# One GpSimd power for the roots of keys and queries, and output weights whose loads are written ahead of their splits

## The chip, the cores and the metric

The kernel runs on one core of one Trainium2 chip. The metric is device time in microseconds; lower is better. In the profile the engines are PE (TensorE, matrix products), PEld (its weight loads), DVE (VectorE), ACT (ScalarE), POOL (GpSimd) and SP (SyncE, which issues most DMAs).

## The reference

One decoder layer is computed for a prompt group (512 tokens behind 16 meta tokens) and a sample group (8 sequences of 8 tokens with 2048 cached positions each). Differential attention and a gated delta rule read the same projection of the normalised input; their outputs are projected, gated, merged and sent through one output projection; a gated feed-forward part follows. All is float32. What the change touches, cut to its core:

```
def l2norm(x):
    return x * rsqrt(sum(x * x, axis=-1) + 1e-6)

gq = l2norm(gq) * GDN_DK ** -0.5          # queries of the delta rule, 4 heads of 128
gk = l2norm(gk)                           # keys
...
mix = sigmoid(gate_a) * (o_a @ w_branch_a) + sigmoid(gate_b) * (o_b @ w_branch_b)
x = x + rmsnorm(mix @ w_out, ln_mix_post)
```

## The kernel before, in words

Every product in float32 is built from three rounded ones: a weight tile is loaded raw, ScalarE casts it to its high part, DVE subtracts that for the low part (`split`, lines 314 to 316), and PE multiplies high by high, high by low and low by high (line 273 records all of them). Raw tiles (`wraw`, 128x512) come through SP's queue into three buffers in rotation (`load_w`, lines 308 to 312).

The work is written as two streams of generators that a planner merges by the PE work that each has used: `main` makes the prompt attention and then the delta rule head by head (`gdn`), `rest` makes the sample attention over the cached pages, the sixteen gates and one branch projection (`branch_a`). What the streams emit is then ordered once more for every engine, by when its operands are expected. So the order in which the program is written and the order in which an engine finds its instructions are two things. Each engine works off its own order strictly.

The delta rule of a head (`gdn_chain`, heads counted 0 to 3) starts at the scaling of keys and queries. The keys are transposed to rows (`kn`) and ScalarE sums the squares of keys and queries into `gss`, ten columns: five for the keys, five for the queries, of which columns 0 to 3 are the four chunks of the prompt and column 4 is the tail of 80 rows (samples and meta tokens). `rsqrt` (lines 382 to 385) is a scaling on DVE and a power of -0.5 on GpSimd; it was called once for the keys and once for the queries, into the halves of `grr`. From the keys' half DVE makes `kc` (line 811) and scales `kn` with it (line 814 for the tail, 815 for the chunks); from the queries' half it makes `cq` (line 813). PE then transposes `kn` back (line 421), the Gram products follow, DVE solves the blocks of sixteen (`gdn_base`, lines 953 to 1009, whose results are `xyt` for the tail and `xy` for the chunks), and PE goes on from those. At the same time the next head's projection is convolved on DVE (`cy`, lines 670 to 672, ended by a tanh on ScalarE). `er` (line 833) is the queries times their decays, `vn` (lines 801 and 806) the scaled values, `zk` and `grhs` small copies for later.

The output weights: `branch_a` and `mix` call `wout_ahead` (lines 1560 to 1563) behind each of their steps. It loads a quarter of the first half of `w_out` as two raw tiles and splits them at once into `owhi` and `owlo`. Each step of `branch_a` and `mix` also takes one raw tile for its own branch weights. `out_proj` loads the second half in the same manner.

Of the kernel before, what the change touches and what calls it, by code (L numbers as in the profile page):

```python
# [29 lines left out]
EPS = 1e-6  # L30
# [121 lines left out]
class Body:  # L152
# [39 lines left out]
    def run(self):  # L192
# [13 lines left out]
        with ExitStack() as sm:  # L206
            with ExitStack() as s1:
# [3 lines left out]
                with ExitStack() as s2:  # L211
# [12 lines left out]
                        self.gdn_consts(tmp)  # L224
                    self.news = self.chain = self.spare = False

                    swo, self.wo0, self.wo_next = ExitStack(), [], 0

                    def main():
                        head = {}  # L230
# [503 lines left out]
    def gdn_chain(self, h, st):  # L734
        nc, pool, a, o = self.nc, self.gpool, self.a, self.o
        q, kt, vt = st["q"], st["kt"], st["vt"]
# [43 lines left out]
        ss = self.t(pool, [128, 2, 5], "gss")  # L780
# [24 lines left out]
            self.transpose(pv[:, i], vt[:, 128 * i : 128 * i + 128])  # L805
        nc.vector.tensor_tensor(out=vn[:, 0:4], in0=pv, in1=cols(self.hsb), op=ALU.mult)
        rr = self.t(pool, [128, 2, 5], "grr")
        for e in range(2):
            self.rsqrt(rr[:, e], ss[:, e], 0.25, EPS, 128, 5)
        kc = self.t(pool, [128, 5], "kc")  # L810
        nc.vector.tensor_tensor(out=kc, in0=rr[:, 0], in1=self.hsb[:, :, h], op=ALU.mult)
        cq = self.t(pool, [128, 5], "cq")
# [6 lines left out]
        p = self.ps("t")  # L819
# [3 lines left out]
        p = self.ps4("t")  # L823
# [25 lines left out]
        p = self.ps("g")  # L849
# [13 lines left out]
        p = self.ps("g")  # L863
# [4 lines left out]
        p = self.ps("g")  # L868
# [3 lines left out]
        p = self.ps("g")  # L872
# [26 lines left out]
        for i in range(4):  # L899
            sl = slice(128 * i, 128 * i + 128)  # L900
            p = self.ps("g")
# [9 lines left out]
            p = self.ps("g")  # L911
# [4 lines left out]
            p = self.ps("g")  # L916
# [5 lines left out]
            p = self.ps("g")  # L922
# [18 lines left out]
        p = self.ps4("t")  # L941
# [4 lines left out]
        for dst, src in (((0, SEQ), p.rearrange("p c t -> p (c t)")), ((CS, CM), pt[:, 0:NS]), ((CM, NQ), pt[:, 78:80])):  # L946
            sl = slice(*dst)
# [610 lines left out]
        yield 2.0  # L1558

    def wout_ahead(self):  # L1560
        if self.wo0 and self.wo_next < 4:
            self.load_wout(self.wo0, 0, self.wo_next)
            self.wo_next += 1

    def mix(self):
# [15 lines left out]
    def wout_tiles(self, pool, half):  # L1581
        return tuple(self.t(pool, [128, 8, 512], f"ow{part}{half}", F32R) for part in ("hi", "lo"))

    def load_wout(self, wo, half, q):
        hi, lo = wo
        sl = slice(128 * q, 128 * q + 128)
        for k in (0, 4):
            raw = self.load_w(self.a["w_out"][0][128 * k : 128 * k + 512, 512 * half + 128 * q : 512 * half + 128 * q + 128])
            self.split(hi[:, k : k + 4, sl], lo[:, k : k + 4, sl], raw)

    def out_proj(self, pool, wo0, swo, sm):
        nc, a, f = self.nc, self.a, self.f
# [691 lines left out]
```

## Time and profile before

| | us |
|---|---|
| median of 3 runs | 1135.75 |
| lowest and highest | 1135.46, 1139.98 |
| the profiled execution | 1136.37 |
| its span, first to last instruction | 1134.6 |
| busy: PE, DVE, ACT, POOL | 1112.5, 729.3, 524.7, 225.8 |

The profiled execution took 1.8 us more than its span, which lies around the instructions, and 0.6 us more than the median. A row of a view of instructions has the start in us from the span's start, the duration in us, engine, line, operation, output and inputs, shapes, how many of a kind were merged, and in brackets how long the engine had stood idle before it and what ended that. Rows with three numbers in ns give the shortest, middle and longest duration of a group. Since PE is busy nearly throughout, what is looked for is the rest: the places where it waits.

### The profile page before, as it was taken

Reading aid. Unit: us, or ns where it says so; the run is one execution under the profiler, and the core shown is the slowest. Engines: PE = TensorE matmul, PEld = TensorE weight load, DVE = VectorE, ACT = ScalarE, POOL = GpSimd, SP = SyncE. Lnnn points to the kernel's source line nnn. Section 1 sums busy time; section 2 is a strip of 40 time slices with the busy share of each in tenths; the row PEclk is TensorE's granted clock in tenths of the full one; section 3 lists DMA queues with packets and bytes.
Section 4 is the critical chain, followed back from the end, with each engine's and each line's share of the span. In section 5 each row is a group of like instructions: output and inputs, shape, how many; then the busy total and the mean of one; then the engine's idle time right before and its main releaser. Section 6 shows DMA issues by size and latency. Waiting matters only on the chain.

```text
span 1134.6 us, 22730 instructions
## 1 busy us (share of the span) xinstructions
PE 1112.5 (98%) x8263; PEld 976.8 (86%) x8263; DVE 729.3 (64%) x1891; ACT 524.7 (46%) x1264; POOL 225.8 (20%) x344
## 2 busy tenths in 40 slices
PE   8999999999999999999999999999999999999997
PEld 6987887787787787689999987899999999988886
DVE  5456666696486377375335575599999999752315
ACT  5244544464365365352324244464555555842311
POOL 3122221020120020010000003344444454300000
PEclk9999999999999999999999999999999999999999
DMA  6376336837846866733234344333333332333213
GB/s 193 83 235 199 102 92 200 261 103 251 246 147 224 283 178 223 251 87 87 50 90 118 105 146 135 102 102 95 94 95 95 95 100 84 116 108 108 84 48 120
DMA packets 167610, 156.97 MB, mean 138 GB/s; under 512 B 12540, under 2 KB 123715, under 8 KB 167498
## 3 DMA queue, kind: packets, MB, share of 16 engines
q1 hardware_dynamic: 162833, 147.14, 42.5%
q0 software_dynamic: 3264, 5.16, 1.5%
q10 hardware_dynamic: 1400, 3.22, 0.9%
q8 instruction: 65, 1.06, 0.4%
q14 instruction: 48, 0.39, 0.1%
HBM read 145.60 MB, written 9.88 MB: 137 GB/s over the span
## 4 chain that ended last, share of the span: by engine, by line
PE 82%; DVE 7%; issue 3%; ACT 3%; POOL 3%; DMA 2%; SPq 0%; DVEq 0%; POOLq 0%; ACTq 0%
PE ps_d L273 32%; PE ps_t L273 20%; PE ps_g L273 16%; PE ps_s L273 7%; PE ps_t L421 6%; ACT KT L1421 1%; PE ps_m L273 1%; DVE wlo L316 1%; DVE cy L672 1%; POOL grr L385 1%; DMA wraw<-in_w_ffn_in 1%; DMA page<-in_cache_v 0%; DVE gf L1745 0%; DVE fy L1926 0%; DVE row L992 0%
## 5 line engine op out<-in xcount | busy, mean ns | idle before, releaser
L273 PE MATMUL ps_d<-xhi,whi 128*128 128x256 f32 (+2 forms) x704 | 217.3, 309 | 0.6 <-ACT xhi L315 0.5
L273 PE MATMUL ps_d<-xhi,wlo 128*128 128x256 f32 (+2 forms) x704 | 213.0, 303 | 0.5 <-POOL wlo L316 0.5
L273 PE MATMUL ps_d<-xlo,whi 128*128 128x256 f32 (+2 forms) x704 | 212.4, 302 | 0.3 <-DVE xlo L316 0.3
L316 DVE TENSOR_TENSOR wlo<-wraw,whi 128x512 fp32r<-128x512 f32 x190 | 143.5, 772 | 107.2 <-ACT whi L315 106.3
L315 ACT CAST whi<-wraw 128x512 fp32r<-128x512 f32 x194 | 116.5, 621 | 163.7 <-PE ps_d L273 69.4
L273 PEld LDWEIGHTS ps_d<-xhi,whi 128*128 128x128 f32 x704 | 133.1, 189 | 6.2 <-issue 3.8
L273 PEld LDWEIGHTS ps_d<-xlo,whi 128*128 128x128 f32 x704 | 133.4, 190 | 3.2 <-issue 2.4
L273 PEld LDWEIGHTS ps_d<-xhi,wlo 128*128 128x128 f32 x704 | 133.2, 189 | 2.4 <-issue 1.0
L316 DVE TENSOR_TENSOR lw<-sw,hw 128x512 fp32r<-128x512 f32 x76 | 69.8, 918 | 5.2 <-ACT hw L315 5.2
L1421 ACT COPY KT<-ps_t 128x512 f32<-128x512 f32 x106 | 57.2, 603 | 31.6 <-PE ps_t L421 31.1
L421 PE MATMUL ps_t<-consts,page 128*128 128x128 f32 x512 | 67.8, 279 | 0.5
L273 PE MATMUL ps_t<-fhit,hw 128*128 128x290 f32 x228 | 68.1, 299 | 0.1
L273 PE MATMUL ps_t<-flot,hw 128*128 128x290 f32 x228 | 67.7, 297 | 0.0
L273 PE MATMUL ps_t<-fhit,lw 128*128 128x290 f32 x228 | 67.7, 297 | 0.0
L421 PEld LDWEIGHTS ps_t<-consts,page 128*128 128x128 f32 x512 | 55.5, 140 | 14.1 <-issue 7.0
L315 ACT CAST hw<-sw 128x512 fp32r<-128x512 f32 x76 | 46.7, 617 | 18.5 <-PE ps_g L273 12.2
L273 PEld LDWEIGHTS ps_t<-fhit,hw 128*128 128x128 f32 x228 | 43.0, 189 | 0.4 <-DVE p L1949 0.4
L273 PEld LDWEIGHTS ps_t<-flot,hw 128*128 128x128 f32 x228 | 43.3, 190 | 0.0
L273 PEld LDWEIGHTS ps_t<-fhit,lw 128*128 128x128 f32 x228 | 43.1, 189 | 0.0
L1924 ACT ACTIVATE fy<-fpre,fw 128x592 f32<-128x592 f32 x22 | 19.5, 884 | 46.3 <-DVE fpre L1884 46.3
L1926 DVE SCALAR_TENSOR_TENSOR fy<-fpre,fw,fy 128x592 f32<-128x592 f32 x44 | 36.5, 829 | 1.0 <-ACT fy L1924 0.3
L273 PE MATMUL ps_s<-page,pT 128*32 128x256 f32 x512 | 35.1, 385 | 2.0 <-DMA page<-in_cache_v 1.8
(691 smaller groups left out, 2870.0 us busy)
## 6 DMA issues: line engine op xcount, KB each, us to landing
page<-in_cache_k SPq DMA_DIRECT2D x128, 256.0 KB, 4.4
page<-in_cache_v SPq DMA_DIRECT2D x128, 256.0 KB, 4.2
wraw<-in_w_in SPq DMA_DIRECT2D x88, 256.0 KB, 3.1
wraw<-in_w_ffn_in SPq DMA_DIRECT2D x50, 256.0 KB, 3.0
wraw<-in_w_down SPq DMA_DIRECT2D x44, 256.0 KB, 2.8
raw<-in_w_ffn_in SPq DMA_DIRECT2D x38, 256.0 KB, 2.9
wraw<-in_w_out SPq DMA_DIRECT2D x16, 256.0 KB, 3.2
x<-in_x_prompt SPq DMA_DIRECT2D x4, 512.0 KB, 6.8
```

Of the source, the lines that this page charges most:

```text
L273: return self.nc.tensor.matmul(out, lhsT, rhs, **kw).ins
L315: self.nc.scalar.copy(hi, raw)
L316: (eng or self.nc.vector).tensor_tensor(out=lo, in0=raw, in1=hi.bitcast(F32), op=ALU.subtract)
L385: nc.gpsimd.tensor_tensor(out=dst, in0=dst, in1=self.mhalf[:rows, :n], op=ALU.pow)
L421: self.nc.tensor.transpose(out, in_, self.ident[:k, :k])
L672: nc.vector.scalar_tensor_tensor(out=y, in0=pre[:, j : j + n], scalar=self.cw[:, ch, 24 + j : 25 + j], in1=y, op0=ALU.mult, op1=ALU.add)
L1421: copy(kt[:, :, 128 * j : 128 * j + 128], tp)
L1924: nc.scalar.activation(y, pre[:, 0:592], AF.Identity, bias=fw[:, m, 19:20], scale=fw[:, m, 16:17])
L1926: nc.vector.scalar_tensor_tensor(out=y, in0=pre[:, j : j + 592], scalar=fw[:, m, 16 + j : 17 + j], in1=y, op0=ALU.mult, op1=ALU.add)
```

## The change

Two edits. The first calls `rsqrt` once on all ten columns instead of twice on five. The second separates the loads of the output weights from their splits: a step now splits the two raw tiles that the step before had asked for, and then asks for the next two; one step more is needed in all, so the count goes to five. `out_proj` keeps load and split together.

```
-        for e in range(2):
-            self.rsqrt(rr[:, e], ss[:, e], 0.25, EPS, 128, 5)
+        self.rsqrt(rr.rearrange("p e c -> p (e c)"), ss.rearrange("p e c -> p (e c)"), 0.25, EPS, 128, 10)
...
     def wout_ahead(self):
-        if self.wo0 and self.wo_next < 4:
-            self.load_wout(self.wo0, 0, self.wo_next)
+        if self.wo0 and self.wo_next < 5:
+            self.split_wout(self.wo0, self.wo_raws)
+            self.wo_raws = self.load_wout(0, self.wo_next) if self.wo_next < 4 else []
             self.wo_next += 1
...
-    def load_wout(self, wo, half, q):
-        hi, lo = wo
-        sl = slice(128 * q, 128 * q + 128)
-        for k in (0, 4):
-            raw = self.load_w(self.a["w_out"][0][128 * k : 128 * k + 512, 512 * half + 128 * q : 512 * half + 128 * q + 128])
-            self.split(hi[:, k : k + 4, sl], lo[:, k : k + 4, sl], raw)
+    def load_wout(self, half, q):
+        c0 = 512 * half + 128 * q
+        return [(q, k, self.load_w(self.a["w_out"][0][128 * k : 128 * k + 512, c0 : c0 + 128])) for k in (0, 4)]
+
+    def split_wout(self, wo, raws):
+        for q, k, raw in raws:
+            self.split(*(e[:, k : k + 4, 128 * q : 128 * q + 128] for e in wo), raw)
...
-            self.load_wout(wo[1], 1, q)
+            self.split_wout(wo[1], self.load_wout(1, q))
```

What the engines get of it: the second edit changes no row of any engine's order, neither the loads on SP nor the casts on ScalarE nor the subtractions on DVE, and no row waits for another engine or queue than before. The first edit moves rows at the four heads. On DVE at head 0, from the first conv operation of the next tile to the scaled keys, before:

```order
L670 TENSOR_SCALAR cy_3445<-pre_3434,cw_666 128x616
L384 TENSOR_SCALAR grr_3460<-gss_3335 128x5
L811 TENSOR_TENSOR kc_3465<-grr_3460,hsb_635 128x5
L672 SCALAR_TENSOR_TENSOR cy_3445<-pre_3434,cw_666,cy_3445 128x616
L813 TENSOR_SCALAR cq_3467<-grr_3460 128x5
L814 TENSOR_SCALAR kn_3337<-kn_3337,kc_3465 80x128
L672 SCALAR_TENSOR_TENSOR cy_3445<-pre_3434,cw_666,cy_3445 128x616
L815 TENSOR_TENSOR kn_3337<-kn_3337,kc_3465 128x512
```

and with the change:

```order
L384 TENSOR_SCALAR grr_3460<-gss_3335 128x10
L832 TENSOR_TENSOR er_3311<-q_2267,er_3311 128x576
L672 SCALAR_TENSOR_TENSOR cy_3445<-pre_3434,cw_666,cy_3445 128x616
L810 TENSOR_TENSOR kc_3463<-grr_3460,hsb_635 128x5
L812 TENSOR_SCALAR cq_3465<-grr_3460 128x5
L672 SCALAR_TENSOR_TENSOR cy_3445<-pre_3434,cw_666,cy_3445 128x616
L813 TENSOR_SCALAR kn_3337<-kn_3337,kc_3463 80x128
L672 SCALAR_TENSOR_TENSOR cy_3445<-pre_3434,cw_666,cy_3445 128x616
L814 TENSOR_TENSOR kn_3337<-kn_3337,kc_3463 128x512
```

The product er, which stood behind the scaled keys, now stands right behind the scaling, and one cy more stands ahead of the keys; the scaling of the keys' five columns, six rows ahead of the first row shown before, is gone. At head 1 the copy tailT moves from between cq and kn to just behind the scaling, and a small copy (zk) stands between cq and kn instead. At head 2 the keys' scaling stood ahead of er and the queries' one three rows later, behind vn (line 801) and a cy; the one now stands behind er, vn and that cy, and tailT follows it. On DVE at head 3, from the values to the scaled keys, before:

```order
L384 TENSOR_SCALAR grr_7284<-gss_7208 128x5
L811 TENSOR_TENSOR kc_7289<-grr_7284,hsb_635 128x5
L801 TENSOR_SCALAR vn_7211<-ps_t_7245,hsb_635 80x128
L384 TENSOR_SCALAR grr_7284<-gss_7208 128x5
L814 TENSOR_SCALAR kn_7210<-kn_7210,kc_7289 80x128
L815 TENSOR_TENSOR kn_7210<-kn_7210,kc_7289 128x512
L813 TENSOR_SCALAR cq_7291<-grr_7284 128x5
L316 TENSOR_TENSOR wlo_7495<-wraw_7490,whi_7494 128x512
```

and with the change:

```order
L801 TENSOR_SCALAR vn_7205<-ps_t_7239,hsb_635 80x128
L384 TENSOR_SCALAR grr_7278<-gss_7202 128x10
L858 COPY grhs_7941<-vn_7205 16x128
L316 TENSOR_TENSOR wlo_7487<-wraw_7482,whi_7486 128x512
L810 TENSOR_TENSOR kc_7281<-grr_7278,hsb_635 128x5
L812 TENSOR_SCALAR cq_7283<-grr_7278 128x5
L813 TENSOR_SCALAR kn_7204<-kn_7204,kc_7281 80x128
L814 TENSOR_TENSOR kn_7204<-kn_7204,kc_7281 128x512
```

vn, a small copy and one subtraction of weights have moved ahead of kc. On PE the one move of more than two products is behind the blocks of head 1, where ps_s is a score of the sample attention and ps_d the projection for the next head. Before:

```order
L273 MATMUL ps_d_5802<-xhi_6_84,wlo_5796 128x256
L273 MATMUL ps_d_5802<-xhi_6_84,whi_5795 128x256
L273 MATMUL ps_s_5155<-KT_5233,qb_315 32x256 x4
L273 MATMUL ps_s_5155<-KT_5217,qb_315 32x256 x4
L421 MATMUL ps_t_5274<-consts_66,xyt_4936 80x80
L273 MATMUL ps_t_5279<-consts_66,xy_4938 128x32 x4
```

and with the change:

```order
L273 MATMUL ps_d_5798<-xhi_6_84,wlo_5792 128x256
L421 MATMUL ps_t_5270<-consts_66,xyt_4932 80x80
L273 MATMUL ps_d_5798<-xhi_6_84,whi_5791 128x256
L273 MATMUL ps_s_5151<-KT_5229,qb_315 32x256 x4
L273 MATMUL ps_s_5151<-KT_5213,qb_315 32x256 x4
L273 MATMUL ps_t_5275<-consts_66,xy_4934 128x32 x4
```

The transposition of xyt has moved ahead of one projection product and eight scores; xy has stayed behind them. On GpSimd the two powers of a head are one row at the same place.

More of the change, by code (lines that the diff above doesn't have):

```diff
@@ L225, in run @@
                     self.news = self.chain = self.spare = False
-                    swo, self.wo0, self.wo_next = ExitStack(), [], 0
+                    swo, self.wo0, self.wo_next, self.wo_raws = ExitStack(), [], 0, []
                     def main():
```

## The prediction

> **What bounds the kernel now.** First the page's busy times and its chain of waits:
>
> ```profile
> PE 1112.5 (98%) x8263; PEld 976.8 (86%) x8263; DVE 729.3 (64%) x1891; ACT 524.7 (46%) x1264; POOL 225.8 (20%) x344
> PE 82%; DVE 7%; issue 3%; ACT 3%; POOL 3%; DMA 2%; SPq 0%; DVEq 0%; POOLq 0%; ACTq 0%
> ```
>
> TensorE (PE) is busy for 1112.5 of 1134.6 us, so everything that can ever be saved without removing products is its idle time, about 22 us. An edit counts only by the idle time of PE that it adds or takes away. Where that may be I read from the busy times by stage (the columns are PE, weight loads, VectorE (DVE), ScalarE, GpSimd (POOL)):
>
> ```profile
> 230.00:260.00 30.00, 29.85 (x258) 25.57 (x260) 28.81 (x86) 19.82 (x61) 6.26 (x13) 1.00 0.38 123
> 510.00:595.00 85.00, 85.00 (x648) 82.69 (x647) 36.62 (x115) 27.83 (x74) 2.70 (x3) 1.00 0.30 76
> 595.00:680.00 85.00, 84.39 (x593) 80.63 (x592) 51.31 (x90) 33.06 (x61) 0.00 (x0) 1.00 0.42 122
> ```
>
> Where the first head's roots are taken (230 to 260 us) DVE is nearly as full as PE, 28.81 of 30. After the last head's roots PE has no idle time at all (85.00 of 85), so what PE loses or wins before 510 us arrives at the end undiminished. The granted clock is 1.00 in all three.
>
> **The output weights: nothing.** Their stage is 595 to 690 us. ScalarE does wait for these loads, but PE does not:
>
> ```profile
>   DMA wraw<-in_w_out: 10.8, 11
> PE ps_d L273 <- DVE gt L1534: 0.6, 1, 0.6
> ```
>
> The first row is ScalarE's idle time before its casts of w_out, 10.8 us in 11 waits; the second is the only wait of PE between 590 and 690 us. So a perfect early load would be worth at most 0.6 us. And the edit does not even do that: the rows of every engine in this stage are the same in both kernels, one by one (tile numbers apart): the order in which the program is written is not the order in which the engines get it. The 16 loads on SP's queue, the 16 casts on ScalarE and the 16 subtractions on DVE stand at the same places, between the same branch weights, waiting for the same engines. With three raw buffers in rotation, a load cannot start before its buffer is free, wherever the program writes it. Cost: 0, both ways.
>
> **The roots: the price of one power of ten columns.** The trace has no power of ten columns. It has these:
>
> ```profile
> L385 POOL TENSOR_TENSOR r<-r,mhalf x10: 546/554/927, 5.5 to 738.1; 128x1 f32<-128x1 f32 x8, 80x1 f32<-80x1 f32 x1, 66x1 f32<-66x1 f32 x1
> L385 POOL TENSOR_TENSOR grr<-grr,mhalf x8: 1162/1203/1797, 239.4 to 501.7; 128x5 f32<-128x5 f32 x8
> L554 POOL TENSOR_TENSOR sqb<-beta,half x1: 3543/3543/3543, 52.3 to 52.3; 128x20 f32<-128x20 f32 x1
> ```
>
> One column takes 0.55 us, five 1.16 at the least, twenty 3.54. The bounds for ten are therefore 1.16 and 3.54. From one to five a column costs (1.16 - 0.55)/4 = 0.15, from five to twenty (3.54 - 1.16)/15 = 0.16. I take 1.16 + 5 x 0.16 = 1.97 us. The Trainium skill (GPSIMD Engine Reference, section 3.1) gives about 2.6 cycles an element at 1.2 GHz for two-input elementwise work. Estimated from that page, five more columns would cost 11 ns and a power of ten still 1.2 us; the 0.15 us a column of this trace does not bear it out for a power, and it is kept as a rival below.
>
> The longest of the eight is 1.80 us. When it is long shows in the third head:
>
> ```profile
> 417.54 0.75 DVE L833 TENSOR_TENSOR er<-q,er 128x576 f32<-128x576 f32 x1
> 417.71 2.92 POOL L385 TENSOR_TENSOR grr<-grr,mhalf 128x5 f32<-128x5 f32 x2 [2.21 <-DVE grr L384]
> 419.47 1.17 POOL L385 TENSOR_TENSOR grr<-grr,mhalf 128x5 f32<-128x5 f32 x1
> 419.46 0.86 DVE L672 SCALAR_TENSOR_TENSOR cy<-pre,cw,cy 128x616 f32<-128x616 f32 x1
> ```
>
> Of the pair, the second took 1.17 us and so the first 2.92 - 1.17 = 1.75. The first began 0.17 us behind a DVE product with two operands in SBUF and was 0.57 us late; the second began together with one and was not. So I add 0.57 us where DVE already runs such an operation.
>
> Now head by head: when the scaled keys (kn, line 815) are ready before and after, and when PE wants them. Steps between DVE starts come from these rows of the first head: 0.08 for a five-column operation, 0.19 for the small kn, 0.77 for cy, 0.68 to the end of kn.
>
> ```profile
> 240.51 0.18 DVE L384 TENSOR_SCALAR grr<-gss 128x5 f32<-128x5 f32 x1
> 241.97 0.17 DVE L813 TENSOR_SCALAR cq<-grr 128x5 f32<-128x5 f32 x1 [0.33 <-POOL grr L385]
> 242.05 0.27 DVE L814 TENSOR_SCALAR kn<-kn,kc 80x128 f32<-80x128 f32 x1
> 242.24 0.85 DVE L672 SCALAR_TENSOR_TENSOR cy<-pre,cw,cy 128x616 f32<-128x616 f32 x1
> 243.01 0.68 DVE L815 TENSOR_TENSOR kn<-kn,kc 128x512 f32<-128x512 f32 x1
> 245.08 0.67 PE L421 MATMUL ps_t<-consts,kn 80*128 80x80 f32 x5
> ```
>
> *Head 0.* Before, kn is ready at 243.69 and PE takes it at about 245.2: no wait. After, the wide scaling stands at 240.43 (0.08 earlier, a small one ahead of it is gone), the power starts 0.25 later as in the other heads and ends at 242.65; kc, cq, cy, small kn, cy, kn follow in the new order and end at 245.26. PE loses 0.1. But er now stands right behind the scaling, as at 417.54, so I count the 0.57 here: **+0.7**. Queued on DVE behind the waiting kc are the cy of the next conv tile and the tail copy, for which ScalarE's tanh waits; they come some 0.2 later and PE's loss covers them.
>
> ```profile
> 326.00 0.23 DVE L384 TENSOR_SCALAR grr<-gss 128x5 f32<-128x5 f32 x2
> 329.22 0.17 DVE L813 TENSOR_SCALAR cq<-grr 128x5 f32<-128x5 f32 x1 [0.98 <-POOL grr L385]
> 329.54 0.27 DVE L814 TENSOR_SCALAR kn<-kn,kc 80x128 f32<-80x128 f32 x1
> 329.95 0.26 PE L421 MATMUL ps_t<-consts,kn 80*128 80x80 f32 x1 [1.24 <-DVE kn L814]
> ```
>
> *Head 1.* Here PE really waits, 1.24 us, for kn, and DVE's order makes kn wait for the second power as well, since cq stands ahead of it. After: scaling 326.00, power 326.25 to 328.22, kc 328.26, cq, one small copy, kn at 328.52 instead of 329.54: **-1.0**. What is late next is the same transposition, for 0.2 us. But later in this head the order of PE changes too: the transposition of xyt moves ahead of nine products.
>
> ```profile
> 354.20 0.28 PE L273 MATMUL ps_d<-xhi,whi 128*128 128x256 f32 x1
> 354.78 0.24 DVE L998 TENSOR_TENSOR xyt<-xc,consts 80x80 f32<-80x80 f32 x1
> 355.56 0.27 PE L421 MATMUL ps_t<-consts,xyt 80*80 80x80 f32 x1
> 355.77 1.05 PE L273 MATMUL ps_t<-consts,xy 128*128 128x32 f32 x8
> ```
>
> xyt is ready at 355.02, and PE would now want it at 354.20 instead of 355.56. It stands still until 355.06, then does the nine products (ps_d and ps_s, 1.1 us) and comes to xy at about 356.35 instead of 355.77: **+0.6**. DVE and PE are earlier by the same 1.0 here, so that this does not depend on it.
>
> ```profile
> 418.46 0.85 DVE L672 SCALAR_TENSOR_TENSOR cy<-pre,cw,cy 128x616 f32<-128x616 f32 x1
> 421.72 0.68 DVE L815 TENSOR_TENSOR kn<-kn,kc 128x512 f32<-128x512 f32 x1
> 422.29 0.88 PE L421 MATMUL ps_t<-consts,kn 80*128 80x80 f32 x5
> 417.63 0.19 ACT L800 ACTIVATION_READ_ACCUMULATOR gjunk<-ps_t 80x1 f32 x1
> ```
>
> *Head 2.* Before, the keys' root began at 417.45 without the queries' sums. After, vn stands ahead and waits for ScalarE's last sum (417.82), cy follows (418.11), the scaling comes at 418.88, the power runs 419.13 to 421.10, then kc, cq, cy, small kn, and kn ends at 422.94 instead of 422.40. PE wants it at 422.4: **+0.5**.
>
> ```profile
> 499.81 0.19 ACT L800 ACTIVATION_READ_ACCUMULATOR gjunk<-ps_t 80x1 f32 x1
> 501.69 0.68 DVE L815 TENSOR_TENSOR kn<-kn,kc 128x512 f32<-128x512 f32 x1
> 502.52 0.67 PE L421 MATMUL ps_t<-consts,kn 80*128 80x80 f32 x5
> 503.43 0.17 DVE L813 TENSOR_SCALAR cq<-grr 128x5 f32<-128x5 f32 x1 [1.06 <-POOL grr L385]
> ```
>
> *Head 3.* Before, kn came from the first power alone and ended at 502.37, just ahead of PE; the second power (awaited at 503.43) held up only cq and two weight subtractions. After, vn waits for the last sum (500.00), the scaling is at 500.29, the power 500.54 to 502.51, kn ends at 503.58. PE loses **+0.9**. One weight subtraction, with both operands in SBUF, now starts with the power; I count its 0.57 too: **+1.5**.
>
> The four scalings fewer on DVE (4 x 0.08 us) lie beside PE's work and count nothing; if that cover were gone they would be worth 0.3 us. Other swaps on PE move one or two products among independent ones; the only wait of that kind in the trace is 0.2 us (for dtbig_up), and I cost them at 0.
>
> Sum: 0.7 - 1.0 + 0.6 + 0.5 + 1.5 = **+2.3 us** on the profiled execution: 1136.4 becomes 1138.7, and the median of the runs shown, 1135.75, becomes **1138.0**. As a formula: +1.1 on time (0.1 - 1.0 + 0.6 + 0.5 + 0.9), and 4 us for each us by which the power is longer than 1.97.
>
> **The rivals.**
> A. A power of ten costs what five cost (1.18 us). Against it speak the three rows of powers. Heads 0 and 2 then lose nothing, head 1 gains its whole wait of 1.24, xyt costs 0.6, head 3 about 0.1: -0.5, 1135.2 us.
> B. Slower: the power is starved by DVE through a whole row of operations (er and cy back to back, copy and subtraction) and takes as long as twenty columns, 3.5 us. Then 1.1 + 4 x 1.5 = +7.1, 1142.9 us. It decides, beyond 0.5%, from 3.1 us a power on. For it: kn's wait hangs on this one instruction in all heads. Against: the longest delay seen is 0.6 us.
> C. The reverse: a power that began first holds DVE off until it ends. Then in heads 1 and 2 the cy behind the scaling (0.77) comes after the power instead of beside it: +2.3 + 1.5 = 3.8, 1139.6 us. Against it: cy at 419.46 took its usual 0.86 beside a power. The Trainium skill (SBUF — State Buffer, section "Who interferes with whom") says so: the port pair that the two share goes to whichever starts first for its whole instruction, and the other fully blocks. By that rule the longer power would cost DVE more, 3.8 in the sum; the late power at 417.71 agrees with it, the unhindered cy at 419.46 does not.
> D. The losses are absorbed, since PE and the chain wait for each other further on: 0, 1135.8 us. Against it: PE's 85.00 of 85 behind head 3.
> E. The output weights do arrive earlier and take away PE's 0.6: 1137.4 us. The unchanged orders speak against it.
>
> **How the numbers follow.** Forecast 0.62, A 0.08, B 0.07, C 0.10, D 0.08, E 0.05. The range goes from A with the xyt stall missing as well (-1.1, 1134.6) to C with all four powers late (1.1 + 4 x 0.57 + 1.5 = 4.9, 1140.7): 1134.5 to 1141.0, leaving out B. Half a per cent is 5.7 us, about what a measurement of this kernel can tell from no change. Only B reaches it, with a margin for what I do not see: slower 0.08, faster 0.02, same 0.90.
>
> **What would show it.** Right: four powers of 128x10 near 2.0 us, or 2.5 in heads 0 and 3; PE waiting for kn 0.2 us in head 1 and 0.5 to 1.5 in heads 0, 2 and 3; a new wait of PE for xyt near 0.8; ScalarE still idle about 11 us before the casts of w_out. Wrong: powers above 3 us, PE waits for kn in none of the heads, or any difference behind 595 us other than a shift.

## The result, and the profile after

The changed kernel takes **1141.03 us** (median of 8 runs, 1139.82 to 1142.91); the kernel before, run beside it, 1136.7 (8 runs, 1135.46 to 1139.98). The ratio is 1.004 with a 95% interval of 1.003 to 1.0051, so +4.5 us with an interval of 3.4 to 5.8. The forecast was +2.3 and 1138.0; 1141.03 lies just beyond the range's upper end of 1141.0. The kernel before stood at 1135.75 in the three runs from which the forecast was counted and at 1136.7 beside the changed kernel; as a difference the range reached +5.25, and +4.5 lies inside it. The sign and the place were right, the size was not. The profiled execution after took 1140.78 us with a span of 1139.0, 4.4 more than that of before.

First the page's busy times and chain of waits, to be held against the first two lines of the prediction:

```profile
PE 1113.4 (98%) x8263; PEld 976.6 (86%) x8263; DVE 729.2 (64%) x1887; ACT 524.8 (46%) x1264; POOL 224.5 (20%) x340
PE 80%; DVE 7%; issue 5%; ACT 3%; POOL 2%; DMA 2%; SPq 0%; DVEq 0%; POOLq 0%; ACTq 0%
```

PE's idle time grew from 22.1 to 25.6 us, which is 3.5 of the 4.4; the other 0.9 stand in the records as longer busy time, and 0.6 of them are found below, in head 0. The three stages of before, in the same columns:

```profile
230.00:260.00 30.00, 28.83 (x238) 24.30 (x238) 27.00 (x75) 17.92 (x57) 8.42 (x11) 1.00 0.33 98
510.00:595.00 85.00, 85.00 (x652) 82.69 (x651) 38.15 (x119) 28.23 (x74) 2.69 (x3) 1.00 0.29 72
595.00:680.00 85.00, 84.46 (x608) 81.58 (x608) 52.38 (x93) 30.92 (x60) 0.00 (x0) 1.00 0.39 114
```

In the first head PE lost 1.0 us (28.83 busy instead of 29.85). Behind the last head it is as full as before, so what had been lost arrives at the end. The output weights' waits, of ScalarE and of PE between 590 and 690 us (total, times, longest):

```profile
ACT owhi L315 <- DMA wraw<-in_w_out: 10.0, 11, 2.2
PE ps_d L273 <- DVE gt L1533: 0.5, 1, 0.5
```

That is the stage of before, shifted: ScalarE still waits in eleven casts, PE once. The loss is in the roots. The four powers, head 0 to 3:

```profile
240.74 3.19 POOL L385 TENSOR_TENSOR grr<-grr,mhalf 128x10 f32<-128x10 f32 x1 [0.70 <-DVE grr L384]
328.29 2.71 POOL L385 TENSOR_TENSOR grr<-grr,mhalf 128x10 f32<-128x10 f32 x1 [4.51 <-DVE grr L384]
421.58 2.72 POOL L385 TENSOR_TENSOR grr<-grr,mhalf 128x10 f32<-128x10 f32 x1 [3.62 <-DVE grr L384]
504.38 1.98 POOL L385 TENSOR_TENSOR grr<-grr,mhalf 128x10 f32<-128x10 f32 x1 [12.82 <-DVE grr L384]
```

The forecast was 2.5, 2.0, 2.0, 2.5. And PE's waits for what depends on them:

```profile
246.69 0.63 PE L421 MATMUL ps_t<-consts,kn 128*128 128x128 f32 x4 [1.17 <-DVE kn L814]
331.71 0.26 PE L421 MATMUL ps_t<-consts,kn 80*128 80x80 f32 x1 [0.95 <-DVE kn L813]
425.68 0.26 PE L421 MATMUL ps_t<-consts,kn 80*128 80x80 f32 x1 [0.80 <-DVE kn L813]
507.03 0.26 PE L421 MATMUL ps_t<-consts,kn 80*128 80x80 f32 x1 [0.51 <-DVE kn L813]
356.85 0.24 PE L421 MATMUL ps_t<-consts,xyt 80*80 80x80 f32 x1 [0.72 <-DVE xyt L997]
```

Before there was one wait for kn, 1.24 us; now there are four, 3.4 us together, and the new one for xyt.

Why is a power on time in head 3 and late in head 1? DVE's rows around them (two of head 0, two of head 1, one of head 3):

```profile
240.57 0.75 DVE L832 TENSOR_TENSOR er<-q,er 128x576 f32<-128x576 f32 x1
241.24 0.85 DVE L672 SCALAR_TENSOR_TENSOR cy<-pre,cw,cy 128x616 f32<-128x616 f32 x1
...
328.11 0.27 DVE L662 COPY tailT<-ps_t 27x128 f32<-27x128 f32 x1
328.31 0.84 DVE L672 SCALAR_TENSOR_TENSOR cy<-pre,cw,cy 128x616 f32<-128x616 f32 x1
...
504.58 0.69 DVE L316 TENSOR_TENSOR wlo<-wraw,whi 128x512 fp32r<-128x512 f32 x1
```

In head 1 cy begins 0.02 us *behind* the power (328.31 against 328.29) and ends at 329.15; the power ends at 331.00, 1.85 later. The copy ahead of it (tailT) reads PSUM. In head 3 wlo begins 0.20 behind the power, and the power takes 1.98. In head 0 the power ends 1.84 us behind the end of cy (242.09), the second operation of the row. DVE itself is not slowed: 0.84 and 0.69 are its usual durations. The first theory read from this: a power does nothing while DVE works through SBUF in an operation that ran when the power started, or started almost with it.

### The profile page after: what moved, and what is told of

Same layout as the page of the kernel before. It is cut to its first block, busy times and chain, and to the rows that moved or that the text cites. A ratio compares the mean times of both kernels' runs of the same rounds, so it can differ in the third digit from the quotient of the medians.

```text
span 1139.0 us, 22721 instructions
## 1 busy us (share of the span) xinstructions
PE 1113.4 (98%) x8263; PEld 976.6 (86%) x8263; DVE 729.2 (64%) x1887; ACT 524.8 (46%) x1264; POOL 224.5 (20%) x340
## 4 chain that ended last, share of the span: by engine, by line
PE 80%; DVE 7%; issue 5%; ACT 3%; POOL 2%; DMA 2%; SPq 0%; DVEq 0%; POOLq 0%; ACTq 0%
PE ps_d L273 30%; PE ps_t L273 19%; PE ps_g L273 16%; PE ps_s L273 7%; PE ps_t L421 6%; PE ps_m L273 1%; POOL grr L385 1%; ACT KT L1420 1%; DMA wraw<-in_w_out 1%; DVE wlo L316 1%; DVE cy L672 1%; DVE lw L316 1%; DVE row L991 0%; DVE row L992 0%; DMA page<-in_cache_v 0%
```

## The experiments

Each experiment is shown with its edit, its expectation word for word, and what it gave. Single profiled executions of the same rows can differ by some us, so besides the ratio I read one stretch in each trace: from the first row below, a root just ahead of head 0, to the second, the last root of the output norm behind head 3. Before, then after:

```profile
227.35 0.57 POOL L385 TENSOR_TENSOR hss<-hss,mhalf 8x1 f32<-8x1 f32 x1 [4.41 <-DVE hss L384]
588.98 1.19 POOL L385 TENSOR_TENSOR gf<-gf,mhalf 128x5 f32<-128x5 f32 x1 [0.24 <-DVE gf L384]
```

```profile
227.39 0.57 POOL L385 TENSOR_TENSOR hss<-hss,mhalf 8x1 f32<-8x1 f32 x1 [4.41 <-DVE hss L384]
593.54 1.19 POOL L385 TENSOR_TENSOR gf<-gf,mhalf 128x5 f32<-128x5 f32 x1 [0.24 <-DVE gf L384]
```

361.63 us before and 366.15 after: +4.5, the whole difference. All kernels against the kernel before, in us (ratio and interval turned into us with 1137):

| kernel | by ratio | interval | stretch | powers in heads 0 to 3 |
|---|---|---|---|---|
| changed | +4.5 | 3.4 to 5.8 | +4.5 | 3.19, 2.71, 2.72, 1.98 |
| e1_roots | +5.3 | 3.6 to 7.0 | +5.2 | 3.19, 2.71, 2.72, 1.98 |
| e2_wout | +0.9 | -0.7 to 2.4 | +0.8 | as before |
| e3_pair | +5.6 | 3.8 to 7.4 | +5.7 | pairs: 3.55, 3.07, 3.08, 2.33 |
| e9_er_behind | +4.9 | 3.1 to 6.7 | +4.6 | 2.57, 1.98, 2.01, 1.98 |
| e10_vn_behind | +5.0 | 3.1 to 6.9 | +3.8 | 2.78, 2.77, 2.78, 1.95 |
| e4_wide20 | +13.0 | 10.7 to 15.1 | +11.3 | 4.77, 4.29, 4.30, 3.56 |
| e8_keysfirst | +2.4 | 1.0 to 3.8 | +2.5 | pairs: 3.55, 3.07, 3.07, 2.33 |
| e7_behind | -2.6 | -3.9 to -1.4 | -1.3 | as before |
| e7_again | -0.6 | -1.7 to 0.7 | -1.4 | as before |

### Which half of the change: e1_roots, e2_wout

e1_roots is the kernel before with the change's two lines on `rsqrt`; e2_wout is the kernel before with all the other lines of the change.

> The kernel before with the change to the roots alone; every engine gets the same rows as in the changed kernel. Theory (T): the whole loss is the roots': four powers of 128x10, late where a DVE operation with two operands in SBUF runs at their start (3.2, 2.7, 2.7 and 2.0 us in heads 0 to 3), and 4.4 us more than the kernel before, ratio 1.004. Rival (W): the output weights carry part of it; then this kernel loses clearly less, 2 us or so, the 2.3 of the prediction with no late power.

> The kernel before with the change to the output weights alone; every engine gets the same rows as in the kernel before. T: nothing, ratio 1.000, within 0.1% (1.1 us), ScalarE idle some 11 us before its casts of w_out as before. W: a loss of 1 to 2 us, with PE waiting between 595 and 690 us.

e1_roots gave ratio 1.0047 (1.0032 to 1.0062), with the same four powers to 0.01 us; e2_wout 1.0008 (0.9994 to 1.0021). The roots carry all that can be measured, and the output weights are worth nothing either way, as the unchanged rows said. The profiled execution of e2_wout had a span of 1139.1, longer than that of the kernel before by as much as the changed one's, with every row at the same place; 2.0 us of it came ahead of the stretch and 1.7 behind it. That is why one span proves little here.

### Is it the length of the one power? e3_pair, e8_keysfirst, e4_wide20

e3_pair, against the changed kernel (the scaling of ten columns stays):

```
-        self.rsqrt(rr.rearrange("p e c -> p (e c)"), ss.rearrange("p e c -> p (e c)"), 0.25, EPS, 128, 10)
+        flat = rr.rearrange("p e c -> p (e c)")
+        nc.vector.tensor_scalar(flat, ss.rearrange("p e c -> p (e c)"), 0.25, EPS, op0=ALU.mult, op1=ALU.add)
+        for e in range(2):
+            nc.gpsimd.tensor_tensor(out=rr[:, e], in0=rr[:, e], in1=self.mhalf[:, :5], op=ALU.pow)
```

> The changed kernel, but the one power of ten columns is two of five again, keys first; one scaling of ten as in the change, DVE's and PE's orders those of the change, so cq still stands ahead of kn and kn waits for the second power. T: what costs is that both roots begin only when the queries' sums are there and that kn waits for both; the pair ends 2.4 us after its start when on time and 2.9 when its first half is late by 0.57, against 2.0 to 3.2 for the one power. kn is 0.3 us earlier in head 0 and 0.2, 0.2 and 0.4 later in heads 1 to 3: 0.5 us more than the changed kernel, +4.9 on the kernel before. Rival (L): the length of the single instruction is what costs, and the pair brings most of it back: +1 or less.

e8_keysfirst, against e3_pair:

```
-        cq = self.t(pool, [128, 5], "cq")
-        nc.vector.tensor_scalar(cq, rr[:, 1], 0.5 * 128.0**-0.5, None, op0=ALU.mult)
         nc.vector.tensor_scalar(kn[:NTL, 4], kn[:NTL, 4], kc[:NTL, 4:5], None, op0=ALU.mult)
-        nc.vector.tensor_tensor(
+        end = nc.vector.tensor_tensor(
             out=kn[:, 0:4], in0=kn[:, 0:4], in1=kc[:, 0:4].unsqueeze(2).to_broadcast(C4), op=ALU.mult
         )
+        cq = self.t(pool, [128, 5], "cq")
+        with self.tc.issue_after(end.ins):
+            nc.vector.tensor_scalar(cq, rr[:, 1], 0.5 * 128.0**-0.5, None, op0=ALU.mult)
```

> The changed kernel with two powers of five in place of the one, keys first, and cq held behind the wide kn: one scaling of ten as in the change, but kn waits for the keys' power alone. T: this power takes 1.16 us in head 3, about 1.9 in heads 1 and 2 and 2.4 in head 0 (1.05 us behind the end of the DVE row that runs at its start), 0.8 us less than the one power in every head; kn is 0.8 us earlier and 3.2 of the 4.4 us come back: +1.2 on the kernel before (what is left is the wait for the queries' sums in heads 2 and 3). Rival (S): the one scaling, and with it the wait for the queries' sums, is what costs; then little comes back: +3 to +4.

e4_wide20, against the changed kernel (ten columns of ones are added that nobody reads):

```
-        ss = self.t(pool, [128, 2, 5], "gss")
+        ss = self.t(pool, [128, 4, 5], "gss")
...
-        rr = self.t(pool, [128, 2, 5], "grr")
-        self.rsqrt(rr.rearrange("p e c -> p (e c)"), ss.rearrange("p e c -> p (e c)"), 0.25, EPS, 128, 10)
+        rr = self.t(pool, [128, 4, 5], "grr")
+        self.rsqrt(rr.rearrange("p e c -> p (e c)"), ss.rearrange("p e c -> p (e c)"), 0.25, EPS, 128, 20)
```

> The changed kernel with ten more columns of ones (never read) in the sums and roots: the power is 128x20, everything else and its order as in the change (one product on PE trades places in head 0). T: the power takes 1.56 us more in each head (3.54 when on time, 4.7 in head 0, 4.3 in heads 1 and 2), kn comes as much later, and PE, which already waits for kn in all four heads, waits all of it: 4 x 1.56 = 6.2 us more than the changed kernel, +10.6 on the kernel before. Rival (D): PE makes part of it good between the heads; then clearly less, +6 to +8.

The pair instead of the one power is no cure: +5.6, as the theory (T) had it (+4.9), and not the rival's +1. As long as kn waits for both roots, two instructions are no better than one. When kn waits for the keys' half alone (e8_keysfirst) the loss falls to 2.4 (1.0 to 3.8), twice what was expected but within the interval. So of e3_pair's 5.6 some 3.2 are kn's wait for both roots. The rest comes with the one scaling and the orders that follow from it; 0.6 of it is a move of two products on PE, told in the section on the prediction, and what remains was not taken apart.

e4_wide20 is the dose. Its powers are longer by 1.58 us in each head; the stretch grew by 6.8 over the changed kernel's where 6.2 was expected, and PE waits for the small kn in all four heads:

```profile
PE ps_t L421 <- DVE kn L813: 8.5, 4, 2.5
PE ps_t L421 <- DVE kn L814: 1.2, 1, 1.2
```

9.7 us against 3.4 in the changed kernel, +6.3. So the prediction's formula, 4 us for each us by which the power is longer, holds in PE's waits for kn. The 6.8 of the stretch are not as good a proof as they look, since two other things are in them. The granted clock dropped at head 3. From the last products of head 2 to the Gram products of head 3, the changed kernel and then e4_wide20 (columns as in the stages above; the granted clock is the third number from the end):

```profile
488.68:509.89 21.21, 19.09 (x139) 17.28 (x138) 15.32 (x44) 12.44 (x42) 3.91 (x4) 1.00 0.36 91
491.93:516.19 24.26, 20.57 (x139) 18.73 (x138) 15.40 (x44) 12.43 (x42) 5.49 (x4) 0.93 0.33 83
```

The same 139 products took 1.5 us longer at a clock of 0.93. In the other direction, the changed kernel's 0.6 in head 0 (the two products just named) is missing here, because this kernel's order on PE differs by that. The ratio gives more still, 13.0 (10.7 to 15.1) against 10.6, and its interval just misses that; the clock over the whole run was 0.997, 0.994, 0.994 and 0.993 in the four runs of this kernel, against 0.997 to 0.999 in those of the changed one. That the lower clock makes the rest of the difference fits, but is not shown.

### What holds a power up: e5_powers, e11_rows, e12_kinds, e13_head

These four leave the layer out. GpSimd takes nothing but powers, each behind one small scaling on DVE, and behind that stands a given row of DVE operations, five times for each case:

```
+    nc.vector.tensor_scalar(x, src[:, 0:n], 0.25, EPS, op0=ALU.mult, op1=ALU.add)
+    nc.gpsimd.tensor_tensor(out=x, in0=x, in1=half[:, 0:n], op=ALU.pow)
+    for e, op in enumerate(ops):
+        op(e)
+    nc.vector.tensor_tensor(out=out[:, 0:n], in0=x, in1=half[:, 0:n], op=ALU.mult)
```

> The layer is left out; GpSimd takes only powers, five of each case, each behind one small scaling on DVE, with a given row of DVE operations behind that scaling. Theory (T): a power makes no way while DVE is in an unbroken row of operations with two SBUF operands that runs when it starts (or within some 0.03 us), and needs 1.85 us (ten columns) or 1.05 (five) from the end of that row; without one it takes 0.55, 1.16, 1.98 and 3.54 us for 1, 5, 10 and 20 columns. With a row of n operations of 0.77 us each behind the scaling, ten columns take 2.5 us for n = 1, 3.3 for 2 and 4.8 for 4; with a short copy out of PSUM ahead of one such operation 2.7; with operations that read PSUM 2.0. Five columns behind one operation 1.75; pairs of five 2.35 quiet, 2.85 behind one, 5.2 behind four. Rival (F), the prediction's: a fixed delay of about 0.6 us at the start, whatever follows: 2.5 for one, two and four alike, the pair 2.9 behind four. Rival (G): GpSimd's own state decides: all cases of one width alike.

The groups of e5_powers (times of five powers together, then the mean in ns): without an operation of DVE, then behind two operations that read PSUM, then behind four of the form of cy:

```profile
L2286 POOL TENSOR_TENSOR quiettwenty<-quiettwenty,half 128x20 f32<-128x20 f32 x5 | 17.7, 3531 | 2.4 <-DVE quiettwenty L2283 2.4
L2286 POOL TENSOR_TENSOR quietfive<-quietfive,half 128x5 f32<-128x5 f32 x5 | 5.8, 1169 | 2.3 <-DVE quietfive L2283 2.3
L2286 POOL TENSOR_TENSOR bankten<-bankten,half 128x10 f32<-128x10 f32 x5 | 9.8, 1953 | 2.3 <-DVE bankten L2283 2.3
L2286 POOL TENSOR_TENSOR fourten<-fourten,half 128x10 f32<-128x10 f32 x5 | 12.5, 2492 | 5.3 <-DVE fourten L2283 5.3
```

Ten columns on time cost 1.95 here and 1.95 to 2.01 in the layer: the prediction's 1.97 from its three rows of five, one and twenty columns was right. Operations that read PSUM hold nothing up. One cy held ten columns to 2.49 and five to 1.70, as expected; but four of them no longer than one (2.49, expected 4.8). My theory of a whole row fell there, unless it was the short pause between those four, each of which read what the one ahead had written. So e11_rows took independent ones, and one that starts later and later behind the power:

> The layer is left out; only powers of ten columns on GpSimd, five of each case, behind one small scaling on DVE that is followed by a given row of operations. In the run of powers before, the operations of a row read what the one ahead had written, stood 0.90 us apart for a duration of 0.85, and rows of one, two and four were alike, 2.49 us. Here they are independent and should stand 0.77 apart. Theory (T, mended): the power waits for the first pause of DVE between two operations with two SBUF operands, and one of 0.05 us is enough; without a pause it waits for the end of the whole row: 2.5 us for one, 3.3 for two, 4.8 for four independent ones, and 2.5 for two or four chained ones. Rival (F): the delay is one operation's at the most: 2.5 in all these cases (then head 0's 3.2 has another cause). Operations with one SBUF operand, if it is the two that matter: 2.0. One operation that starts 0.04, 0.11, 0.18 and 0.26 us after the power: 2.7, then 2.0 once the power has its operands; by heads 1 and 3 of the changed kernel that lies between 0.02 and 0.2 us. The pair of five behind four independent ones: 5.0 by T, 3.5 by F.

```profile
L2297 POOL TENSOR_TENSOR freefour<-freefour,half 128x10 f32<-128x10 f32 x5 | 12.5, 2494 | 3.8 <-DVE freefour L2294 3.8
L2297 POOL TENSOR_TENSOR singletwo<-singletwo,half 128x10 f32<-128x10 f32 x5 | 10.6, 2115 | 3.1 <-DVE singletwo L2294 3.1
L2297 POOL TENSOR_TENSOR lagc<-lagc,half 128x10 f32<-128x10 f32 x5 | 14.1, 2825 | 2.3 <-DVE lagc L2294 2.3
L2297 POOL TENSOR_TENSOR lagd<-lagd,half 128x10 f32<-128x10 f32 x5 | 9.8, 1954 | 2.3 <-DVE lagd L2294 2.3
```

Four independent operations 0.77 us apart give 2.49 again: the mended theory fell too, and the rival (F), one operation at the most, is right about rows. The later the one operation starts, the longer the power: started 0.09 us behind it (lagb) 2.75, 0.17 behind (lagc) 2.83, and 0.25 behind (lagd) 1.95, not late at all:

```profile
139.47 2.83 POOL L2297 TENSOR_TENSOR lagc<-lagc,half 128x10 f32<-128x10 f32 x1 [0.36 <-DVE lagc L2294]
139.64 0.84 DVE L2272 SCALAR_TENSOR_TENSOR yd<-pre,src,cy 128x616 f32<-128x616 f32 x1
...
155.91 1.96 POOL L2297 TENSOR_TENSOR lagd<-lagd,half 128x10 f32<-128x10 f32 x1 [0.36 <-DVE lagd L2294]
156.16 0.84 DVE L2272 SCALAR_TENSOR_TENSOR ye<-pre,src,cy 128x616 f32<-128x616 f32 x1
```

The rule is then: an operation of DVE that reads SBUF and runs at the power's start, or starts less than 0.2 us behind it (0.17 holds, 0.20 does not), holds the power to that operation's end, and ten columns need 1.81 to 1.85 us from there. lagc: 139.64 + 0.84 + 1.82 = 142.30, and 139.47 + 2.83 is 142.30. An operation with one SBUF operand (singletwo, 0.47 us long) holds too, to its own shorter end. Head 1 by the rule: 328.31 + 0.84 + 1.85 - 328.29 = 2.71, as measured.

The Trainium skill (SBUF — State Buffer, section "Who interferes with whom") names the same operations: those with two SBUF inputs, and those in a two-port mode, which `tensor_scalar` can enter, contend with GpSimd for a port pair that both use; an operation with at most one SBUF input, outside such a mode, does not. The runs agree: 2.49 us behind cy forms, 2.12 behind singletwo, 1.95 behind operations that read PSUM. By the same section of the Trainium skill the pair goes to whichever issues first, for the whole instruction. Here the measurement decides: an operation that the profile shows starting 0.17 us later still holds the power, and no operation of DVE took longer beside a power that had begun first (0.84 in lagd, 0.69 in head 3).

Head 0 remains, where the power waits for the end of the second operation, cy behind er. e12_kinds tried rows of both forms, e13_head the row of head 0 rebuilt:

> The layer is left out, as in the two runs of powers before; five powers of ten columns of each case, now behind rows of plain products (TENSOR_TENSOR, 128x576, 0.75 us, the form of er) and of the cy form (SCALAR_TENSOR_TENSOR, 128x616, 0.85 us, with a scalar from SBUF). Rows of cy forms alone hold the power for the first of them only, 2.49 us. Head 0 of the changed kernel has er and then cy, and 3.19. Theory (K): the power gets in between an operation and a cy form behind a cy form, but not behind a plain product: one plain product 2.4, two 3.05, four 4.4, product then cy 3.2, cy then product 2.5, product then two cy 3.2, and four products ahead of the second half of a pair 3.6 and 1.2. Rival (P): whatever the kind, one operation at the most: 2.4 to 2.5 in all cases, and head 0's 3.19 has another cause, for instance that er or cy waits there on its own operands.

> The layer is left out; powers of ten columns, five of each case, behind the DVE row of head 0 built after the kernel: ahead of the scaling a product that reads PSUM and the first tap of the conv (so that DVE has no pause), behind it the product er in place and the second tap cy, in place, from a column on, with its own scalar. Rival (R): the row does it, and the case with the whole row takes 3.1 to 3.2 us as head 0 does, while the same pair without what stands ahead, or the product or the tap alone, takes 2.4 to 2.5; the cases then show which piece it hangs on. Theory (N): the row does not do it, all cases with a product or tap behind the scaling take 2.4 to 2.5, and the second 0.6 us of head 0 come from something that these kernels lack (other engines and transfers at work).

```profile
L2289 POOL TENSOR_TENSOR ttstt<-ttstt,half 128x10 f32<-128x10 f32 x5 | 12.0, 2392 | 2.4 <-DVE ttstt L2286 2.4
```

```profile
L2300 POOL TENSOR_TENSOR head<-head,half 128x10 f32<-128x10 f32 x5 | 12.0, 2394 | 12.7 <-DVE head L2299 12.7
```

All powers of ten columns behind such rows took 2.39 to 2.55, the pair behind four products 2.9. Theory (K) and rival (R) fell; the 0.8 us more of head 0 (3.19 against 2.39) are not made by the row itself. They are no accident of one trace: e1_roots has 3.19 in head 0 again, and e4_wide20 has 4.77 there against 3.56 on time, 1.21 late like the changed kernel. What makes them stays **open**.

### The rule inside the layer: e9_er_behind, e10_vn_behind

e9_er_behind, against the changed kernel, where end is the wide kn as above:

```
-        nc.vector.tensor_tensor(out=qs[:, 0:CM], in0=q[:, 0:CM], in1=er[:, 0:CM], op=ALU.mult)
+        with self.tc.issue_after(end.ins):
+            nc.vector.tensor_tensor(out=qs[:, 0:CM], in0=q[:, 0:CM], in1=er[:, 0:CM], op=ALU.mult)
```

> The changed kernel with one edit: er, a DVE product with two operands in SBUF, is held behind the wide kn. By the order of the rows, DVE then has one cy instead of er and cy behind the scaling in head 0, and no operation with two SBUF operands behind it in heads 1 and 2 (in heads 1 and 2 only copies and a memset); head 3 as before (a weight subtraction 0.2 us behind the power's start). T: the powers take 2.7 us in head 0 and 2.0 in heads 1, 2 and 3 (the changed kernel: 3.2, 2.7, 2.7, 2.0), kn is earlier by 0.5, 0.7 and 0.7, and about 1.9 us of the 4.4 come back if the other swaps on PE cost nothing: +2.5 on the kernel before. Rival (G): the lateness is GpSimd's own, for instance because it was idle before; then the powers stay at 3.2, 2.7 and 2.7, whatever DVE does, and the time at +4.4.

e10_vn_behind, against the changed kernel:

```
-        nc.vector.tensor_scalar(vn[:NTL, 4], pt[:NTL, 2], self.hsb[:NTL, 4, h : h + 1], None, op0=ALU.mult)
...
-        self.rsqrt(rr.rearrange("p e c -> p (e c)"), ss.rearrange("p e c -> p (e c)"), 0.25, EPS, 128, 10)
+        flat, sums = rr.rearrange("p e c -> p (e c)"), ss.rearrange("p e c -> p (e c)")
+        start = nc.vector.tensor_scalar(flat, sums, 0.25, EPS, op0=ALU.mult, op1=ALU.add)
+        nc.gpsimd.tensor_tensor(out=flat, in0=flat, in1=self.mhalf[:, :10], op=ALU.pow)
+        with self.tc.issue_after(start.ins):
+            nc.vector.tensor_scalar(vn[:NTL, 4], pt[:NTL, 2], self.hsb[:NTL, 4, h : h + 1], None, op0=ALU.mult)
```

> The changed kernel with the small vn (80x128, reads PSUM) written behind the scaling of the sums instead of ahead of it. The order of PE stays but for a few products; ScalarE's, GpSimd's and SP's stay. By the rows, vn then stands between the scaling and the next cy in heads 0, 1 and 2, so that cy starts some 0.09 us after the power instead of 0.02, er is out of the row in head 0, and in heads 1 and 2 the scaling is ahead of one cy and so 1.0 us earlier. Theory (T): 0.09 us is enough for the power to get its operands: 2.0 us in all four heads. kn is then earlier by 1.2 in head 0, 1.0 in heads 1 and 2 (a cy stands between cq and kn there now) and the same in head 3; PE's waits for kn of 1.2, 0.95 and 0.8 go and about 2.9 of the 4.4 us come back: +1.5 on the kernel before. If 0.09 is too short, the powers take 2.7 in heads 0 to 2 and 1.1 come back: +3.3. Rival (G), GpSimd's own state: 3.2, 2.7, 2.7 and 2.0 as before.

The powers of e9_er_behind, head 0 to 3, and the row in which PE takes kn in head 2:

```profile
240.27 2.57 POOL L385 TENSOR_TENSOR grr<-grr,mhalf 128x10 f32<-128x10 f32 x1 [0.70 <-DVE so L838]
327.28 1.98 POOL L385 TENSOR_TENSOR grr<-grr,mhalf 128x10 f32<-128x10 f32 x1 [4.51 <-DVE grr L384]
417.65 2.01 POOL L385 TENSOR_TENSOR grr<-grr,mhalf 128x10 f32<-128x10 f32 x1
504.03 1.98 POOL L385 TENSOR_TENSOR grr<-grr,mhalf 128x10 f32<-128x10 f32 x1 [12.82 <-DVE grr L384]
```

```profile
425.28 0.67 PE L421 MATMUL ps_t<-consts,kn 80*128 80x80 f32 x5
```

The powers did what (T) said, 2.57 and three times 2.0; that GpSimd's own state made them late is ruled out. The time did not: +4.9 instead of +2.5. Counted from the root that begins the stretch, PE was 0.87 us behind the kernel before at the start of head 2 (the changed kernel 2.40), so heads 0 and 1 did give back 1.5. In head 2 it fell behind again: the scheduler had put kn's transposition on PE behind other products, at 425.28, although kn had been ready since 420.78, and its Gram products were 3.75 late. From the last products of head 1 to these Gram products PE stood idle for 2.07 us against 0.39 before, waiting for ScalarE (1.4 us) and other things, but not for kn. One edit moved more than it was meant to; that loss belongs to the new order, not to the powers.

In e10_vn_behind cy starts 0.08 us behind the power, and by lagb (2.75) and lagc that is not enough: the powers took 2.78, 2.77, 2.78, 1.95, and theory (T) fell. The expectation gave +3.3 for this case; the stretch shows +3.8, the ratio 5.0 (3.1 to 6.9).

### A version that is not slower: e7_behind, e7_again

Both are one kernel: the kernel before, with cq held behind the wide kn (the edit shown for e8_keysfirst).

> The kernel before with one edit: cq, which waits for the queries' power, is held behind the wide kn on DVE in every head (before, it stands ahead of kn in heads 0, 1 and 2). No other engine's order changes. T: kn then waits for the keys' power alone, some 1.2 us earlier where cq held it. PE waits for kn before only in head 1 (1.24 us); most of that wait goes: -1.0 on the kernel before, ratio 0.999. Rival: PE then waits for something as late in head 1 and nothing is won, ratio 1.000.

> The kernel before with cq behind the wide kn, a second time, since the first gave -2.6 us (interval -3.9 to -1.4) against an expected -1.0, while in its trace the stretch from the end of the projections to the last root of the output norm (227 to 589 us) is 1.3 us shorter. Theory of the wait for kn alone: -1.0 to -1.4, ratio 0.9988 to 0.9991. Rival: something outside this stretch is won too: -2.5, ratio 0.9978.

PE's wait for kn in the stretch, in e7_behind:

```profile
PE ps_t L421 <- DVE kn L813: 0.3, 1, 0.3
```

It was 1.24. The ratios were 0.9977 (0.9966 to 0.9988) and 0.9995 (0.9985 to 1.0006), the stretch -1.3 and -1.4. A gain of 1.4 us lies in both intervals and at the edge of each; the theory of the wait for kn alone (-1.0 to -1.4) stands, and the -2.6 of the first series was not repeated. It is clearly faster than the changed kernel. Against the kernel before the gain is small, and only the first of the two series shows it clear of noise. It does the opposite of the change: the keys' root is waited for alone.

## Why the prediction was right and where it was wrong

**Right.** The output weights: nothing (0.9994 to 1.0021). The price of ten columns: 1.97 forecast (its own sum, 1.16 + 5 x 0.16, gives 1.96), 1.98 measured on time. That the loss is mostly PE's idle time, 3.5 of 4.4 us, and that it is carried to the end. The formula of 4 us per us of power, in PE's waits for kn. The xyt stall in head 1: 0.8 forecast, 0.72 measured. Waits for kn of 0.5 to 1.5 in heads 0, 2 and 3: 1.17, 0.80 and 0.51; in head 3 that is partly luck, since the late power counted there did not come.

**Wrong** was the delay of the powers, the step "So I add 0.57 us where DVE already runs such an operation". By it heads 1 and 2 were on time, because of the sentence on the pair in head 2: "the second began together with one and was not" late. That one row was taken for the rule. The trace of before had two others that speak against it, in heads 1 and 3:

```profile
326.14 0.85 DVE L672 SCALAR_TENSOR_TENSOR cy<-pre,cw,cy 128x616 f32<-128x616 f32 x1
326.24 2.95 POOL L385 TENSOR_TENSOR grr<-grr,mhalf 128x5 f32<-128x5 f32 x2 [4.51 <-DVE grr L384]
...
501.66 1.74 POOL L385 TENSOR_TENSOR grr<-grr,mhalf 128x5 f32<-128x5 f32 x1 [0.61 <-DVE grr L384]
501.69 0.68 DVE L815 TENSOR_TENSOR kn<-kn,kc 128x512 f32<-128x512 f32 x1
```

In head 1, which was counted as on time, the pair took 2.95 us instead of 2.33, behind a cy that ran at its start. In head 3 the wide kn began 0.03 us *behind* the power, which still waited for its end (502.37) and ended 1.03 after it. So a power is also held by an operation that starts behind it (e11_rows: up to 0.17 us), and then for that operation's whole length. Why the second power of head 2 was on time with cy beside it is not shown; it differs in that no scaling had just released it. The delays forecast were 0.57, 0, 0, 0.57; measured 1.21, 0.73, 0.74, 0: 2.68 us instead of 1.14. In the formula that is 1.1 + 2.68 = 3.8 instead of 2.3. PE's wait for kn in head 1, forecast at 0.2 us, was 0.95 for the same reason.

A second term was put at nothing: "Other swaps on PE move one or two products among independent ones". One of them costs 0.6, in head 0, as the rows below the table show. With it the sum is 1.1 + 2.68 + 0.6 = 4.4, against 4.5 measured.

By head, the lag of PE behind the kernel before, which each head added (starts of the same PE rows in both traces):

| | forecast | measured |
|---|---|---|
| head 0, to its Gram products | +0.7 | +1.4 |
| head 0, from there to xyt | 0 | +0.6 |
| head 1, to kn | -1.0 | -0.3 |
| head 1, xyt and xy | +0.6 | +0.7 |
| head 2 | +0.5 | +1.4 |
| head 3 | +1.5 | +0.7 |
| sum | +2.3 | +4.5 |

Heads 0, 1 and 2 each miss by about their unforecast delay (0.64, 0.73, 0.74). In head 3 the wlo that was counted starts 0.20 behind the power and so holds nothing; from its Gram products (+1.2) to its xyt PE makes up another 0.5. The 0.6 behind head 0's Gram products has no wait of PE beside it. PE's rows there, first before, then after:

```profile
249.03 1.07 PE L273 MATMUL ps_s<-KT,qb 128*32 128x256 f32 x16
255.18 0.64 PE L273 MATMUL ps_s<-KT,qb 128*32 128x256 f32 x8
...
250.50 1.06 PE L273 MATMUL ps_s<-KT,qb 128*32 128x256 f32 x14
252.59 0.62 PE L273 MATMUL ps_s<-KT,qb 128*32 128x256 f32 x2
257.39 1.93 PE L273 MATMUL ps_s<-KT,qb 128*32 128x256 f32 x32
```

Sixteen scores stood together; now two of them stand behind the Gram products of the queries, and those two alone take 0.62 us. From the first Gram product (247.72 and 249.19) to the next scores the same products take 8.20 us instead of 7.46. It is the order that does it: in e4_wide20, where the sixteen stay together, they take 7.51, and in e1_roots, e3_pair and e8_keysfirst, where two are split off, 8.2. Why two scores there cost so much is not shown.

**The rivals.** A (ten cost as five) and D (absorbed) are out by 1.98 and by PE's 85.00 of 85. E is out by e2_wout. C (the power holds DVE off) is out: cy took 0.84 beside a power. B went in the right direction: its ground against it, "the longest delay seen is 0.6 us", fell in head 0 with 1.21, and a power held through more than one operation is seen there alone.

## What to carry to other kernels

Merging two small instructions of a slow engine saves little (here 1.95 to 1.98 us for the one power against 2.33 for the pair, both on time), while the result that is wanted first then waits for both inputs and for both halves: ask which half the bound engine wants, and keep it alone. When a trace gives the delay of an instruction in one neighbourhood, read every other row of its kind in the same trace before making a rule of it, and take as its upper end the whole length of the operation next to it, and not the remainder that was seen. Where a scheduler orders the rows, an edit of one line must be read in the rows of all engines before its time is put down to that line; a move of two products can cost as much as a late power.

## What the runs showed of the hardware

- A power on GpSimd costs 0.55 us for one column, 1.17 for five, 1.95 for ten, 3.53 for twenty.
- A DVE operation that reads SBUF and that the profile shows starting up to 0.17 us behind a power still holds it, for its whole length (2.83 instead of 1.95); from 0.20 us on it does not (1.98).
- Two scores of PE that stand apart from the other fourteen took 0.62 us, where sixteen together took 1.07.
- Behind four independent operations a pair of five columns took 3.18 us instead of 2.30, so the second of a pair is not safe either, though the one in head 2 of the kernel before was on time. Here it began 0.31 us behind such an operation (177.16 against 176.85) and took 1.57 us instead of 1.17. The pair, and its second power alone:

```profile
175.55 3.18 POOL L2297 TENSOR_TENSOR freepair<-freepair,half 128x5 f32<-128x5 f32 x2 [0.56 <-DVE freepair L2294]
177.16 1.57 POOL L2297 TENSOR_TENSOR freepair<-freepair,half 128x5 f32<-128x5 f32 x1
```
